# The mixer's output projection by seven products of eight, with its weight sums made ahead

## The chip, the core and the metric

The kernel runs on one core of one Trainium2 chip. The time is device microseconds of one execution. Five engines work beside each other, each through its own instructions in a fixed order: PE multiplies matrices, DVE and ACT do elementwise work, POOL does a little elementwise work and issues transfers that add into their target, SP issues the other loads. They meet through semaphores: an instruction that waits holds up everything behind it on its engine.

## The reference

One layer of a decoder trunk over 512 tokens of width 2048, each sub-layer with a norm ahead of it and a residual add behind:

```python
x = x + concat(dilated_attention, forgetting_attention, gated_linear_attention) @ w_out
x = x + cross_attention(rms_norm(x), rms_norm(mem)) # 256 memory tokens, 4 heads of 128
x = x + gated_mlp(rms_norm(x))                      # with a causal convolution of width 3
y = rms_norm(x)
```

All of it is float32. The change is in the product with `w_out` (2048 x 2048), in the sum of squares that the next norm needs, and in the preparation of the memory tokens for the cross-attention.

## The kernel before

Tokens lie along the free dimension, 512 of them, and features along 128 partitions: the stream is 16 tiles of 128x512 float32. To keep float32's accuracy each operand is split into a rounded high part and the rest (`whi` and `wlo` for weights: ACT makes the first, DVE the second), and one product is three matmuls: high by high, low by high and high by low (`mm3`, lines 375 to 377). Weights come as 512 KB loads on SP's queue into a ring of five (`wraw`); each load is split in two halves into rings of five `whi` and five `wlo`.

The output projection computes 16 output tiles, each from 16 blocks of the mixer's output: 16 x 3 matmuls of 512 columns a tile. The first four tiles take the first half of their blocks among the last steps of the attention; after it they take the second half, and tiles 4 to 15 follow whole (`out_units`, with `weights` at lines 361 and 362). A finished tile is added to the stream on DVE (`resid`, line 1073), squared on ACT (line 1094) and its square added to one of two sums `sq`, by POOL for even tiles and DVE for odd ones (line 1096; the first two squares by POOL at line 1090). From tile 8 on, each half tile is followed by a step of `memory`: it loads four blocks of memory tokens, splits them with their gain (lines 328 and 329), and adds up their squares in `msq`; its last two steps work out the norm (`stats`) and spread it over the partitions. Then `cross` multiplies the memory tokens by the key weights (PE on `mhi` and `mlo`) and the value weights.

The gated MLP's up projection works with seven products of eight already; sums of its weights that are used late are made ahead, in DRAM, by POOL's transfers: `up_sums(f)` issues eight of 512 KB, most of them adding and waiting for an earlier one. Sets 2 and 3 run in the attention (line 1316), set 1 behind `first_sums` (lines 1362 and 1366) in the cross-attention.

The order in which each engine runs its instructions comes from a scheduler over the program as it is written: it moves an instruction past others of its engine where it expects the engine free, so rows can stand far from where the code has them. On chip every engine then keeps that order.

Of the kernel before, what the change touches and what calls it, by code (L numbers as in the profile page):

```python
# [19 lines left out]
P = 128  # L20
# [33 lines left out]
EARLY = 4  # L54
BELOW = 3 * PHASE
# [28 lines left out]
H0 = 4  # L84
H1 = 6
ST = 4
# [89 lines left out]
def _pack(inp):  # L176
# [26 lines left out]
    a["w_o"] = _units_out(w_out, r(D))  # L203
# [30 lines left out]
class _Trunk:  # L234
# [200 lines left out]
    def stats(self, parts, n, name, pool=None):  # L435
# [8 lines left out]
        rs = self.con.tile([P, tl], F32, name="rs" + name)  # L444
        nc.vector.tensor_scalar(rs, ss[:, :tl], 1.0 / D, EPS, op0=ALU.mult, op1=ALU.add)
        nc.gpsimd.tensor_tensor(rs, rs, self.mhalf[:, :tl], op=ALU.pow)

        def spread():
            bc = self.pst("T")
            for t in range(tl):  # L450
                dg = (pool or self.pre).tile([P, P], F32, name="diag", tag="diag", bufs=tl)
                nc.vector.tensor_scalar(dg, self.ident, rs[:, t:t + 1], None, op0=ALU.mult)
                nc.tensor.matmul(bc[:, t * P:(t + 1) * P], self.ones, dg, start=True, stop=True)
            big = (pool or self.con).tile([P, n], F32, name="R", tag="R", bufs=1)
# [63 lines left out]
    def attend(self, qf, kf, e, vv, bias_of, head, mix):  # L518
# [17 lines left out]
        bias = bias_of(head)  # L536
# [344 lines left out]
    def mixer(self):  # L881
# [95 lines left out]
        for kl, o in zip(self.kl, (slice(DH, P), slice(0, DH))):  # L977
            nc.vector.memset(kl[o].bitcast(F32), 0.0)
        self.up_pre = {}
        for f in range(2, EARLY):  # L980
# [18 lines left out]

        def evac_o(dt):  # L1000
            def f(ps):
                self.resid(dt, ps, None, sqs, lambda n: self.mp.tile([P, n], F32, name="sqt", tag="sqt", bufs=2))
# [10 lines left out]
        units = [self.out_units(d["w_o"], n, xo, evac_o(n), box=box) for n in range(KT)]  # L1013
        self.rate = W_O / 2
        for n in range(0, 4, 2):
# [15 lines left out]
        self.flush()  # L1031
        es_ab.close()
# [4 lines left out]
        for n in range(4):  # L1037
            units[n][1]()
        mem = self.memory()
        for n in range(4, KT):  # L1040
            for u in units[n]:
                u()
                if n >= M0:
                    next(mem, None)
        for _ in mem:
            pass

    def memory(self):

        nc, mp = self.nc, self.mp  # L1050
        parts = [mp.tile([P, MEM], F32, name="msq%d" % i) for i in range(2)]
        self.mem = []
        for k in range(KT):
            if k % 4 == 0:
                four = mp.tile([P, 4, MEM], F32, name="mraw", tag="mraw", bufs=1)
                nc.sync.dma_start(out=four, in_=self.d["memT"][k // 4])
            raw = four[:, k % 4, :]
# [807 lines left out]
```

## Time and profile before

| | us |
|---|---|
| median of three runs | 2252.43 (2251.92 to 2252.64) |
| profiled execution | 2251.13 |
| its span | 2249.3 |
| PE busy | 2232.6 (99%) |
| DVE, ACT, POOL busy | 1819.5, 1231.7, 221.3 |
| window of tiles 4 to 15 | 707 to 837 |
| key units begin | 836.67 |

PE's busy time is nearly the span, so a window's length is what its matmuls take. A matmul's row shows a duration longer than the distance to the next, since matmuls overlap; the distance between starts is what counts. In the rows of DVE the same holds to a small part. Where the profile names the releaser of a wait, it is the one that came last.

### The profile page before, as it was taken

How to read it: one execution, taken by the hardware profiler on the slowest of the kernel's cores; microseconds unless marked ns; L12 is line 12 of the kernel's file. 1: busy time of each engine (PE TensorE's matmuls, PEld its weight loads, DVE VectorE, ACT ScalarE, POOL GpSimd, SP SyncE). 2: the span in 40 equal slices, each digit the busy share in tenths (PEclk: the TensorE clock that was granted, in tenths of full speed). 3: DMA queues.
4: the chain of work that ended last, by engine and by line, in shares of the span. 5: the costliest groups of instructions: out<-in, count | busy, mean ns of one | idle time of the engine just before them, and what ended most of it. 6: DMA issues, size and time to landing. Idle time of an engine off the chain costs nothing.

```text
span 2249.3 us, 42619 instructions
## 1 busy us (share of the span) xinstructions
PE 2232.6 (99%) x15898; PEld 2089.9 (93%) x15898; DVE 1819.5 (81%) x3587; ACT 1231.7 (55%) x2532; POOL 221.3 (10%) x308
## 2 busy tenths in 40 slices
PE   9999999999999999999999999999999999999997
PEld 8898898888888888889999999999999999999997
DVE  7826756666787356699999999999999999989887
ACT  7324445555575245585555555555555575747563
POOL 2000101000002011121111111111000020101003
PEclk9999999999999999999999999999999999999999
DMA  6422157222224359589777777877534493837542
GB/s 223 162 96 82 49 150 193 97 89 99 78 92 140 122 161 241 134 206 282 198 212 201 221 208 213 215 219 224 173 132 144 145 344 104 305 124 233 186 129 82
DMA packets 141842, 377.09 MB, mean 168 GB/s; under 512 B 14484, under 2 KB 53732, under 8 KB 140932
## 3 DMA queue, kind: packets, MB, share of 16 engines
q1 hardware_dynamic: 90144, 274.18, 35.1%
q0 software_dynamic: 45728, 89.86, 18.2%
q10 hardware_dynamic: 5764, 10.35, 1.3%
q8 instruction: 124, 2.03, 0.4%
q14 instruction: 82, 0.67, 0.1%
HBM read 347.28 MB, written 91.80 MB: 195 GB/s over the span
## 4 chain that ended last, share of the span: by engine, by line
PE 96%; DVE 2%; ACT 1%; DMA 0%; issue 0%; POOL 0%; SPq 0%; DVEq 0%; ACTq 0%
PE acc L375 19%; PE acc L377 19%; PE acc L376 19%; PE psC L375 5%; PE psC L376 5%; PE psC L377 5%; PE acc L416 3%; PE acc L418 3%; PE acc L417 3%; PE psD L377 3%; PE psD L376 3%; PE psD L375 3%; PE psT L556 1%; PE psQ L377 1%; PE psQ L375 1%; PE psQ L376 1%
## 5 line engine op out<-in xcount | busy, mean ns | idle before, releaser
L336 ACT ACTIVATE whi<-wraw 128x512 fp32r<-128x512 f32 (+1 forms) x822 | 471.1, 603 | 407.3 <-PE acc L376 145.0
L337 DVE TENSOR_TENSOR wlo<-wraw,whi 128x512 fp32r<-128x512 f32 (+1 forms) x822 | 522.3, 656 | 65.9 <-ACT whi L336 61.2
L375 PE MATMUL acc<-sum,whi 128*128 128x256 f32 x1956 | 541.8, 277 | 0.4 <-ACT s L1465 0.3
L377 PE MATMUL acc<-sum,wlo 128*128 128x256 f32 x1956 | 541.5, 277 | 0.0
L376 PE MATMUL acc<-sum,whi 128*128 128x256 f32 x1956 | 541.4, 277 | 0.0
L362 DVE TENSOR_TENSOR wlo<-wraw,whi 128x512 fp32r<-128x512 f32 (+2 forms) x328 | 216.1, 665 | 191.2 <-ACT whi L361 188.8
L375 PEld LDWEIGHTS acc<-sum,whi 128*128 128x128 f32 x1956 | 367.2, 188 | 1.0 <-ACT s L1465 0.8
L377 PEld LDWEIGHTS acc<-sum,wlo 128*128 128x128 f32 x1956 | 367.3, 188 | 0.4 <-DVE wlo L337 0.2
L376 PEld LDWEIGHTS acc<-sum,whi 128*128 128x128 f32 x1956 | 367.3, 188 | 0.1
L361 ACT ACTIVATE whi<-wraw 128x512 fp32r<-128x512 f32 (+2 forms) x328 | 198.5, 610 | 284.3 <-PE acc L376 186.5
L375 PE MATMUL acc<-xhi,whi 128*128 128x512 f32 (+1 forms) x848 | 335.1, 395 | 0.5 <-ACT fg L926 0.5
L377 PE MATMUL acc<-xhi,wlo 128*128 128x512 f32 (+1 forms) x848 | 328.4, 387 | 0.0
L376 PE MATMUL acc<-xlo,whi 128*128 128x512 f32 (+1 forms) x848 | 327.9, 387 | 0.0
L375 PE MATMUL psC<-sum,whi 128*128 128x256 f32 x928 | 256.9, 277 | 0.0
L376 PE MATMUL psC<-sum,whi 128*128 128x256 f32 x928 | 256.8, 277 | 0.0
L377 PE MATMUL psC<-sum,wlo 128*128 128x256 f32 x928 | 256.5, 276 | 0.0
L377 PEld LDWEIGHTS acc<-xhi,wlo 128*128 128x128 f32 x848 | 159.3, 188 | 32.5
L375 PEld LDWEIGHTS acc<-xhi,whi 128*128 128x128 f32 x848 | 159.4, 188 | 29.9 <-ACT fg L926 0.9
L376 PEld LDWEIGHTS acc<-xlo,whi 128*128 128x128 f32 x848 | 159.7, 188 | 29.0 <-DVE xlo L324 0.2
L377 PEld LDWEIGHTS psC<-sum,wlo 128*128 128x128 f32 x928 | 174.3, 188 | 0.0
L375 PEld LDWEIGHTS psC<-sum,whi 128*128 128x128 f32 x928 | 174.3, 188 | 0.0
L376 PEld LDWEIGHTS psC<-sum,whi 128*128 128x128 f32 x928 | 174.2, 188 | 0.0
(401 smaller groups left out, 4319.0 us busy)
## 6 DMA issues: line engine op xcount, KB each, us to landing
wraw<-in_w_up SPq DMA_DIRECT2D x125, 512.0 KB, 6.3
b<-in_w_up SPq DMA_DIRECT2D x42, 512.0 KB, 4.5
wraw<-in_w_o SPq DMA_DIRECT2D x32, 512.0 KB, 3.5
wraw<-in_w_d SPq DMA_DIRECT2D x32, 448.0 KB, 4.3
wraw<-in_w_d SPq DMA_DIRECT2D x36, 384.0 KB, 5.0
wraw<-in_w_qka SPq DMA_DIRECT2D x24, 512.0 KB, 3.5
up<-in_w_up POOLq DMA_DIRECT2D x24, 512.0 KB, 7.0
one<-in_w_d POOLq DMA_DIRECT2D x24, 448.0 KB, 6.7
```

What stands on the lines that cost most here:

```text
L336: nc.scalar.activation(hi, r, AF.Copy)
L337: nc.vector.tensor_tensor(lo, r, hi.bitcast(F32), op=ALU.subtract)
L361: nc.scalar.activation(hi, r, AF.Copy)
L362: nc.vector.tensor_tensor(lo, r, hi.bitcast(F32), op=ALU.subtract)
L375: nc.tensor.matmul(out, lh, rh, start=start, stop=False, skip_group_check=more)
L376: nc.tensor.matmul(out, lh, rl, start=False, stop=False, skip_group_check=more)
L377: last = nc.tensor.matmul(out, ll, rh, start=False, stop=stop, skip_group_check=more)
L416: self.nc.tensor.matmul(o, xh[:, tt], wh, start=(k == 0), stop=False)
L417: self.nc.tensor.matmul(o, xh[:, tt], wl, start=False, stop=False)
L418: self.last = self.nc.tensor.matmul(o, xl[:, tt], wh, start=False, stop=(k == KT - 1))
L556: nc.tensor.transpose(tp[:, b * P:(b + 1) * P], pt[:, b * P:(b + 1) * P], self.ident)
```

## The change

Four tiles stay as they were. The other twelve are three `quad`s of four tiles. A quad is two pairs of output tiles; a pair is computed from 2 x 2 blocks (two output tiles, halves of the 512 tokens, pairs of input blocks) by seven products instead of eight. Each product is 8 x 3 matmuls of 256 columns. It needs sums of weight blocks and sums of token blocks:

- `out_sums` makes the weight sums in DRAM ahead of time: 32 transfers of POOL, 384x512 (786 KB) each, in the attention, in front of `up_sums` 2, 3 and now also 1.
- `token_turns` makes the token sums: subtractions and splits on DVE and ACT, in steps between the products of the first two quads.
- `quad` multiplies, and puts the products together with adds on DVE and ACT; a tile is ready only after several products, and its residual add goes into a list (`todo`) that is worked off among the next products.
- The squares of these tiles are added to `sq` by an adding transfer of POOL (line 1188) instead of POOL's or DVE's adds.
- `memory` runs among the products of the last quad. It loads two blocks at a time, and the squares from the third on are added into two tiles `low` by adding transfers of POOL (line 1273). `stats` for it is called after the second of the key units, and its last step after the fourth; the keys' evacuations wait in a list until then.
- `attend` issues a head's bias load two heads ahead.

On DVE, at the end of the last quad and the start of the key units (`wlo` of line 344 are weight halves of the quad, of line 369 the key units'; `tok` the split memory tokens; `vg` partial tiles; `low<-low` the add of `stats` over the memory's squares):

```order
1241 L344 TENSOR_TENSOR wlo<-wraw,whi 128x512 [waits DVE_49,DMAHW3_49,PE_49,Activation_49]
1242 L344 TENSOR_TENSOR wlo<-wraw,whi 128x512 [waits PE_49,Activation_49]
1243 L448 TENSOR_TENSOR low<-low 128x256 [waits DMASW4_49,DMASW3_49]
1244 L344 TENSOR_TENSOR wlo<-wraw,whi 128x512 [waits DMAHW7_49,PE_49,Activation_49]
1245 L1168 TENSOR_TENSOR vg<-vg,s_6888 128x256 [waits Activation_49]
1246 L1168 TENSOR_TENSOR vg<-s_6888,acc 128x256 [waits DMASW7_49]
1247 L336 SCALAR_TENSOR_TENSOR xlo<-str,gains,xhi 128x512 [waits Activation_49]
1248 L1168 TENSOR_TENSOR vg<-vg,s_6889 128x256 [waits DVE_49]
1249 L344 TENSOR_TENSOR wlo<-wraw,whi 128x512 [waits PE_49,Activation_49]
1250 L1168 TENSOR_TENSOR str<-xraw,vg 128x512 [waits DMAHW1_49,DVE_49]
```

The add of `stats`, which the code calls in the key units, stands ahead of the quad's last six weight halves, and waits for two transfers of POOL. Before, the same add on DVE:

```order
1108 L329 SCALAR_TENSOR_TENSOR mlo_7586<-mraw,gains,mhi_7585 128x256
1109 L329 SCALAR_TENSOR_TENSOR mlo_7593<-mraw,gains,mhi_7592 128x256 [waits Activation_49]
1110 L1096 TENSOR_TENSOR msq_7367<-msq_7367,msqt 128x256 [waits DVE_49,Activation_49]
1111 L441 TENSOR_TENSOR msq_7366<-msq_7366,msq_7367 128x256 [waits DVE_49,Pool_49]
1112 L362 TENSOR_TENSOR wlo<-wraw,whi 128x512 [waits PE_49,Activation_49]
```

It stood right behind the last square's add of its own engine. On POOL the memory's squares are now these transfers (`low<-spare`), with the stream's (`sq<-vg`) between and behind them:

```order
112 L1273 DMA low<-spare 128x256 [waits DMASW6_49]
113 L1188 DMA sq_6461<-vg 128x512 [waits DMASW7_49,Activation_49]
114 L1273 DMA low<-spare 128x256 [waits DMASW0_49,Activation_49]
115 L1273 DMA low<-spare 128x256 [waits DMASW4_49,DMASW1_49,Activation_49]
116 L1273 DMA low<-spare 128x256 [waits DMASW3_49,Activation_49]
117 L1273 DMA low<-spare 128x256 [waits DMASW4_49,Activation_49]
118 L1273 DMA low<-spare 128x256 [waits DMASW5_49,Activation_49]
119 L1273 DMA low<-spare 128x256 [waits DMASW6_49,Activation_49]
```

Each of them waits for the landing (a semaphore DMASW) of the one two places before it in its kind, as both add into the same tile; before, each place was an add on POOL or DVE that waited for ACT's square.

The diff, with the parts that the prediction speaks of; the token sums' arithmetic is cut:

```diff
+PLAIN = 4
+QUADS = (KT - PLAIN) // 4
+LAST_ORDER = (5, 6, 3, 7, 1, 2, 4)
+OUT_ORDER = (1, 2, 4, 5, 6, 3, 7)
...
     def attend(...):
+            if f is turn and t == 1:
+                n = self.heads.index(me) + 2
+                if n < len(self.heads):
+                    name, h = self.heads[n]
+                    self.biases[name, h] = getattr(self, name)(h)
...
-        for f in range(2, EARLY):
+        self.out_sums()
+        for f in (2, 3, 1):
             self.up_sums(f)
...
-        mem = self.memory()
-        for n in range(4, KT):
-            for u in units[n]:
-                u()
-                if n >= M0:
-                    next(mem, None)
-        for _ in mem:
-            pass
+        mem = self.mem_steps = self.memory()
...
+        for c in range(QUADS):
+            last = c == QUADS - 1
+            if last:
+                next(mem)
+            self.quad(PLAIN + 4 * c, LAST_ORDER if last else OUT_ORDER, mem if last else turns,
+                      c == QUADS - 2)
+        while self.todo:
+            self.todo.popleft()()
+        self.mem_rest = mem
...
+    def quad(self, d0, order, steps, swap):
...
+        def out(o, i):
...
+            tt(x1, raw, t, ALU.subtract if i else ALU.add)
+            nc.scalar.activation(t, x1, AF.Square)
+            nc.gpsimd.dma_start(out=self.sqs[i], in_=t, accum_op=ALU.add)
...
+        for n, j in enumerate(order):
+            for o in pairs:
+                s1, s5 = o["s1"], o["s5"]
+                parts = self.halves(self.up_raw(o["src"][j]))
...
+                ps = bank(o, where[j])
+                for i in range(NP):
+                    th, tl = parts[i // 4]
+                    c = slice(i % 4 * P, (i % 4 + 1) * P)
+                    self.mm3(ps, th[:, c], tl[:, c], *self.operand(j, i), i == 0 and j not in (2, 3, 7),
+                             i == NP - 1, more=True)
...
     def memory(self):
...
+        parts = [self.low(MEM, F32) for _ in range(2)]
         for k in range(KT):
...
+            if k < 2:
+                nc.scalar.activation(parts[k], raw, AF.Square)
+            else:
+                sq = self.spare([P, MEM])
+                nc.scalar.activation(sq, raw, AF.Square)
+                nc.gpsimd.dma_start(out=parts[k % 2], in_=sq, accum_op=ALU.add)
...
     def cross(self):
...
         for i, u in enumerate(first):
             more((i >= H0) + (i >= H1))
+            if i in (2, 4):
+                next(self.mem_rest)
+            if i == 4:
+                ready.append(True)
+                for f, ps in keys:
+                    f(ps)
             u()
...
+    def out_sums(self):
+        w, n = self.d["w_p"], (KT - PLAIN) // 4
+        self.out_src = []
+        for g in range(2):
+            t = [self.dr.tile([n * P, 1024], F32, name="wo%d%d" % (g, i)) for i in range(4)]
+            b11, _, b22, b21 = b = [w[i, g * n:(g + 1) * n].rearrange("k p c -> (k p) c") for i in range(4)]
+            cuts = [slice(512 * h, 512 * (h + 1)) for h in range(2)]
+            self.added(*[[[x[:, c] for c in cuts] for x in y] for y in (t, b)])
```

`added` is the chain that `up_sums` used already: a first copy, then adds into it, each issued behind the one before on POOL's queue; it now takes lists of pieces.

More of the change, by code (lines that the diff above doesn't have):

```diff
@@ L978, in mixer @@
             nc.vector.memset(kl[o].bitcast(F32), 0.0)
+        self.biases = {}
+        self.heads = [("bias_a", h) for h in range(A_HEADS)] + [("bias_b", h) for h in range(B_HEADS)]
         self.up_pre = {}
-        for f in range(2, EARLY):
+        self.out_sums()
+        for f in (2, 3, 1):
             self.up_sums(f)
@@ new lines, in mixer @@
+        self.mem_left = KT // 2
+        for n in range(PLAIN):
+            w = self.weights(d["w_o"][2 * n + 1])
+            for kk in range(8):
+                wh, wl = w(kk * P, P)
+                self.mm3(box[n], wh, wl, *xo[8 + kk], False, kk == 7)
+            if n == PLAIN - 2:
+                turns = self.token_turns([self.mix[m] for m in order], xo)
+                for _ in range(4):
+                    next(turns)
+        for n in range(PLAIN):
+            evac_o(n)(box[n])
+        for c in range(QUADS):
[4 more added lines that the diff above has]
+                      c == QUADS - 2)
@@ L1052, in memory, with load @@
+    def memory(self):
+        nc = self.nc
+        def load(k):
+            two = self.spare([P, 2, MEM])
+            nc.sync.dma_start(out=two, in_=self.d["memT"][k // 4, :, k % 4:k % 4 + 2, :])
+            return two
+        loads = [load(0), load(2)]
         self.mem = []
+        yield
+        parts = [self.low(MEM, F32) for _ in range(2)]
         for k in range(KT):
-            if k % 4 == 0:
-                four = mp.tile([P, 4, MEM], F32, name="mraw", tag="mraw", bufs=1)
-                nc.sync.dma_start(out=four, in_=self.d["memT"][k // 4])
@@ L1057, in memory @@
-            raw = four[:, k % 4, :]
-            hi = mp.tile([P, MEM], F32R, name="mhi%d" % k)
-            lo = mp.tile([P, MEM], F32R, name="mlo%d" % k)
-            self.mem.append(self.split_to(hi, lo, raw, self.gain(4, k)))
-            self.square(k, raw, parts, lambda n: mp.tile([P, n], F32, name="msqt", tag="msqt", bufs=2))
-            if k % 4 == 3:
+            if k % 2 == 0:
+                two = loads.pop(0)
+            raw = two[:, k % 2, :]
+            both = self.ring()
+            self.mem.append(self.split_to(both[:, :MEM], both[:, MEM:], raw, self.gain(4, k)))
@@ L1116, in evac_k @@
             return f
[L1118 to L1119 removed]
+        ck = [self.spare([P, S], F32R) for _ in range(X_HEADS)]
+        vh = [self.spare([P, S], F32R) for _ in range(MT)]
+        vl = [self.spare([P, S], F32R) for _ in range(MT)]
         def evac_v(t, ps):
```

221 lines of the change are left out of this document (179 added, 42 removed).

## The prediction

> **What bounds the kernel now.** I read the page's busy time and chain first, then a table of stages, then the groups, the timeline and the queues of the stages that the change touches.
>
> ```profile
> span 2249.3 us, 42619 instructions
> PE 2232.6 (99%) x15898; PEld 2089.9 (93%) x15898; DVE 1819.5 (81%) x3587; ACT 1231.7 (55%) x2532; POOL 221.3 (10%) x308
> PE 96%; DVE 2%; ACT 1%; DMA 0%; issue 0%; POOL 0%; SPq 0%; DVEq 0%; ACTq 0%
> ```
>
> PE is idle for 16.7 us of 2249.3 (2249.3 - 2232.6), and the chain that ended last is 96% PE. So only two things move the end: PE work taken out or put in, and any new time in which PE waits. The stages (window, its length, then busy time of PE, PEld, DVE, ACT, POOL, the granted clock, the DMA engines' share, GB/s):
>
> ```profile
> 307.00:395.00 88.00, 87.78 (x443) 75.17 (x441) 56.20 (x139) 48.68 (x108) 13.26 (x17) 1.00 0.73 192
> 604.00:690.00 86.00, 85.69 (x429) 69.98 (x427) 70.58 (x203) 56.11 (x137) 0.00 (x0) 1.00 0.26 90
> 707.00:837.00 130.00, 130.00 (x580) 107.84 (x579) 58.48 (x93) 50.42 (x90) 15.63 (x16) 1.00 0.42 143
> 837.00:854.00 17.00, 17.00 (x143) 16.81 (x142) 14.88 (x26) 13.11 (x23) 1.04 (x1) 1.00 1.02 270
> 1010.00:1800.00 790.00, 789.60 (x6935) 789.21 (x6934) 754.90 (x1225) 439.95 (x789) 80.66 (x105) 1.00 0.69 199
> ```
>
> The twelve tiles of the change are 707 to 837: PE is full there and DVE idle for more than half of it, the shape in which fewer products should pay. The memory's key units follow (837 to 854), PE full again, so a delay made before them isn't made up behind.
>
> **The change part by part.**
>
> *Fewer products.* The spacing of matmuls, from PE's timeline where the last tile of 512 columns ends and the key units of 256 begin (start, duration):
>
> ```profile
> 834.63 0.39 PE L375 MATMUL acc<-xhi,whi 128*128 128x512 f32 x1
> ...
> 836.67 0.28 PE L375 MATMUL acc<-mhi,whi 128*128 128x256 f32 x1
> ...
> 841.15 0.28 PE L377 MATMUL acc<-mhi,wlo 128*128 128x256 f32 x1
> ```
>
> Nine of 512 columns lie between the first two rows: 2.04/9 = 226.7 ns. Before, 12 tiles x 16 x 3 = 576 of them: 130.6 us. Now 3 quads x 14 products x 8 x 3 = 1008 of 256 columns. For their spacing there are two rows: the long up stage of 256-column products, 789.60/6935 = 113.9 ns, and the key units, 38 from 836.67 to 841.15, 117.9 ns. I take 113.9, since token sums against split weights are what the up stage multiplies too: 114.8 us. **Gain 15.8 us**; by the key units' spacing it would be 11.8.
>
> *What the products need on DVE and ACT.* A weight half costs PE 12 x 113.9 ns = 1.37 us now. DVE writes per half one `wlo`, and beside it the token sums' subtractions and splits in the first quad. Durations and spacing:
>
> ```profile
> L362 DVE TENSOR_TENSOR wlo<-wraw,whi 128x512 fp32r<-128x512 f32 x48 | 32.7, 687 | 47.2 <-ACT whi L361 47.2
> L361 ACT ACTIVATE whi<-wraw 128x512 fp32r<-128x512 f32 x48 | 30.0, 629 | 69.6 <-PE acc L376 69.5
> L1096 DVE TENSOR_TENSOR msq<-msq,msqt 128x256 f32<-128x256 f32 x4 | 1.6, 412 | 0.0
> L1094 ACT ACTIVATE msqt<-mraw 128x256 f32<-128x256 f32 x8 | 3.2, 402 | 0.0
> 838.18 0.68 DVE L362 TENSOR_TENSOR wlo<-wraw,whi 128x512 fp32r<-128x512 f32 x1
> 838.78 0.74 DVE L329 SCALAR_TENSOR_TENSOR xlo<-str,gains,xhi 128x512 fp32r<-128x512 f32 x1
> 839.44 0.68 DVE L1096 TENSOR_TENSOR sq<-sq,sqt 128x512 f32<-128x512 f32 x1
> 840.05 0.68 DVE L362 TENSOR_TENSOR wlo<-wraw,whi 128x512 fp32r<-128x512 f32 x1
> ```
>
> Operations queued back to back start 0.60 us apart for `wlo`, 0.66 for `xlo`, 0.61 for an add: 0.08 less than their durations, so a 128x256 one goes at about 0.33. In the first quad DVE's order has per half one `wlo` and mostly a 128x256 and a 128x512 of the tokens: 0.60 + 0.33 + 0.60 = 1.53 against 1.37, for some ten halves. The ring of five split halves lends up to 5 x 1.37 = 6.8 us, so between 0 and 3 us show. I take **1 us lost**. ACT's half costs 0.63 and has room.
>
> *Weight sums ahead.*
>
> ```profile
> L1316 POOL DMA_DIRECT2D up<-in_w_up x24: 611/1015/1112, 307.7 to 1590.6; - x24
> 691.67 1.42 POOL L1090 TENSOR_TENSOR sq<-str 128x512 f32<-128x512 f32 x1 [302.42 <-DVE str L1073]
> ```
>
> Before, 16 POOL transfers of 512 KB (8.4 MB, two sets of sums) fill 307.7 to 395; the engines' share rises there from 0.26 (row of 604) to 0.73: 0.47 x 88 = 41 us of all sixteen, 4.9 us per MB. The new 32 transfers move 25.2 MB, 124 us of all sixteen; in the 0.74 that is free, 167 us. Three sets of the up sums follow at 44 us each. End: 307 + 167 + 132 = 606 us. POOL's next work, behind all of these in its queue, is the first square, before at 691.67 after 302.42 us without work. If each 786 KB transfer ran alone at 1.5 x 5.5 us (88/16, scaled by size), it would be 307 + 264 + 132 = 703. DVE needs the squares in its first quad at about 709 (two POOL operations of 1.4 us and an add before that), so even this doesn't show. Slower loads do not either: at 837 to 854 the share was 1.02 and PE was busy for all 17.00 us. Cost 0; its cover is the 85 us between 606 and 691. The biases two heads ahead: PE was idle 0.31 us in 604 to 690, so they are worth nothing.
>
> *Squares by DMA.* The adds of the stream's squares leave POOL and DVE; neither was on the path there (15.63 and 58.48 us of 130), so they are worth nothing by themselves. The memory's fourteen adds become two chains of seven POOL transfers (128x256, 128 KB), each waiting for the one two before it, since they add into the same two tiles. Their sum is read by one DVE add, the first step of `stats`. In DVE's order that add stands behind 22 of the last quad's 28 weight halves: six more `wlo`, the evacuations and the key units' first half are queued behind it. The nearest rows are the stream's accumulating transfers of 128x512 (256 KB) in the cross-attention's output:
>
> ```profile
> L1254 POOL DMA_DIRECT2D sq<-xsqt x14: 862/872/907, 956.0 to 996.6; - x14
> DMA to landing us min/median/max: 3.3/4.7/7.2
> 977.03 0.86 POOL L1254 DMA_DIRECT2D sq<-xsqt  x1 [1.47 <-ACT xsqt L1253]
> 978.58 0.86 POOL L1254 DMA_DIRECT2D sq<-xsqt  x1 [0.68 <-ACT whi L336]
> 983.68 0.87 POOL L1254 DMA_DIRECT2D sq<-xsqt  x1 [4.24 <-DMA sq<-xsqt]
> 986.18 0.87 POOL L1254 DMA_DIRECT2D sq<-xsqt  x1 [1.62 <-DMA sq<-xsqt]
> ```
>
> Where a link waited for its own chain, the period was 983.68 - 977.03 = 6.65 and 986.18 - 978.58 = 7.60 us. Issuing is 0.87 of it and doesn't shrink; half of the rest for half of the bytes gives 3.76 and 4.24. I take **c = 4.0 us** a link, since these two rows are the only ones of two chains that run against each other. Low end: the least landing, 3.3, halved, with the issue: 2.5. High end: the median landing, 4.7, not shrunk, with the issue: 5.6.
>
> The stall, from t0, PE's start of the last quad (14 products of 2.73 us, so its end is t0 + 38.3). The two tiles of partial sums lie where the quad's first two products read a token sum: free at t0 + 5.5, then an evacuation and two squares on ACT, 0.4 each: first transfer at t0 + 6.7, the second chain 0.9 behind it, the last landing at t0 + 7.6 + 7c. After it DVE has to run, in its order, 7 `wlo` (0.60), 7 operations of 128x256 (0.33), 2 residual adds (0.60) and 6 `xlo` (0.66) before the key units' first half is there: 4.2 + 2.3 + 1.2 + 4.0 = 11.7 us. PE starts the key units at t0 + 19.3 + 7c in place of t0 + 38.3: lost 7c - 19.0, **9.0 us at c = 4.0**, nothing below c = 2.7, 20.2 at c = 5.6. SP is held too: its loads of the later memory blocks wait for links of the chain, and the last three weight loads of the quad stand behind the load that waits for the third link:
>
> ```profile
> wraw<-in_w_o SPq DMA_DIRECT2D x32, 512.0 KB, 3.5
> ```
>
> Freed at t0 + 7.6 + 3c = t0 + 19.6 and landed 3.5 later, they are there well before PE's twelfth product at t0 + 30, so this hides behind the products. DVE has 14.88 of 17 us to do in the key units, so it keeps up there but wins nothing back.
>
> The Trainium skill, "DMA: Bandwidth & Descriptors", section "Anatomy of one DMA — SWDGE (gpsimd) path", fits a transfer as about 2.0 us plus bytes at 436 GB/s. By that, an estimate, a link of 128 KB takes 2.3 us and this sum would hold no stall. For 256 KB it gives 2.6, and the fourteen here landed in 3.3 to 7.2, so this trace does not bear it out.
>
> *Sum.* -15.8 + 1 + 9 = -5.8 us. The profiled execution took 2251.13 (span 2249.3 and 1.8 around it), so 2245.3; the median of the runs, 2252.43, is 1.3 above it: **2246.6 us**.
>
> **The rivals.**
>
> *The chain is short.* If landings are like the quiet ones, c = 2.5, DVE finds the sums there and only the first quad costs: 2252.4 - 15.8 + 0 to 1 = 2237. For it: the share in 707 to 837 is 0.42, and the accumulates were measured in a busier stretch. Against it: this quad loads 512 KB every 2.73 us, 192 GB/s, more than the 143 there, and the two chains contend with each other.
>
> *The chain eats the gain.* Same place: if a link costs what a 256 KB one does (c = 5.6) the loss is 20.2 and the kernel comes out at 2252.4 - 15.8 + 1 + 20.2 = 2257.8, slower. It decides from 7c - 19 = 14.8, c = 4.8: above that the chain takes all that the products gave. For it: medians near 4.7 at twice the size suggest that much of a landing doesn't depend on bytes. Against: the two chain-bound rows scaled as above.
>
> *Half-width products aren't half as long.* At the key units' 117.9 ns the gain is 11.8, the last quad is 39.6 us long and the stall 7.7: 2252.4 - 11.8 + 1 + 7.7 = 2249.3, no change that can be told. For it: those units also have 256 columns against split weights. Against: 6935 records at 113.9.
>
> *The sums arrive late.* From an end of about 706 on, every microsecond holds POOL's squares, then DVE and PE. 32 transfers at 10 us each would end at 307 + 320 + 132 = 759, some 50 us lost: 2290. Nothing in the rows asks for it unless transfers in pairs hinder each other.
>
> **How the numbers follow.** About 0.2%, 4.5 us, is what a measurement here can tell from no change. Forecast (c from 3.4 to 4.6, 2242 to 2251): 0.50. Short chain: 0.22. Long chain: 0.16. Wide spacing: 0.07. Late sums: 0.05. Faster by over 4.5 us, below 2247.9: the short chain and some two thirds of the forecast, 0.56. Within: the other third, the wide spacing and a part of the long chain, 0.27. Slower: the rest of the long chain and late sums, 0.17. The range runs from no stall to c = 5.5: 2237 to 2257; the forecast's own is 2242 to 2251.
>
> **What would show it.** In the trace of the changed kernel: matmuls of the quads 113 to 114 ns apart, and the out projection's PE time near 115 us. One wait on DVE at the memory's sum (`low<-low`), released by a DMA, of some 10 us, and PE idle right behind it, before the key units: about 9 us. The starts of `low<-spare` on POOL two apart by c: 4.0. The weight sums ended near 606 and POOL's first square not later than before. It would be wrong if DVE reaches that add when the chain has landed (c under 2.7), if PE idles in the first quad by more than 3 us, or if the idle time sits in the attention.

## The result and the profile after

The changed kernel takes 2269.55 us (median of six runs, 2264.13 to 2270.98); the kernel before, beside it, 2251.78 us (2251.25 to 2252.64). The ratio is 1.0075, with an interval of 1.0064 to 1.0086: 17.8 us slower. The prediction was 2246.6 us, with a range of 2237 to 2257. The profiled execution of the change is the fastest of its six, 2264.13 us with a span of 2262.3, so its trace holds 13.0 us of the 17.8 (2262.3 - 2249.3).

The page of the changed kernel, its span, busy times and the engines of the chain that ended last:

```profile
span 2262.3 us, 43896 instructions
PE 2228.4 (99%) x16330; PEld 2105.9 (93%) x16330; DVE 1861.5 (82%) x3692; ACT 1266.7 (56%) x2610; POOL 272.0 (12%) x351
PE 61%; DMA 2%; DVE 1%; ACT 1%; issue 0%; POOL 0%; DVEq 0%; ACTq 0%; POOLq 0%
```

PE's busy time fell by only 4.2 us, and its idle time rose from 16.7 to 33.9 us (2262.3 - 2228.4). The chain has 2% of DMA now: work released by a transfer, where before 96% was PE. (Its shares add up to 65% because the profile follows it back from the end to 789.61 us only, into the last quad.)

The points at which PE reaches the same place of the program show where the time went. In the changed kernel PE starts the first quad, the last quad, the memory's key units and the first 512-column product behind the value units at:

```profile
708.81 0.28 PE L382 MATMUL acc<-xhi,whi 128*128 128x256 f32 x1
...
788.78 0.29 PE L382 MATMUL psC<-tok,whi 128*128 128x256 f32 x1
...
848.24 0.29 PE L382 MATMUL acc<-tok,whi 128*128 128x256 f32 x1
...
897.98 0.39 PE L382 MATMUL acc<-xhi,whi 128*128 128x512 f32 x1
```

Before, the twelve tiles and the first 512-column product behind the value units began at

```profile
705.20 0.39 PE L375 MATMUL acc<-xhi,whi 128*128 128x512 f32 x1
...
882.63 0.39 PE L375 MATMUL acc<-xhi,whi 128*128 128x512 f32 x1
```

and the key units at 836.67. Between the first of these rows and the key units lie 576 matmuls of 512 columns, and eight small ones of the memory's norm (four at 775.92, four at 781.81) that take 0.9 us of the first eight tiles. In the changed kernel these eight stand in the key units.

| stretch | before | after | difference |
|---|---|---|---|
| up to the twelve tiles (attention and four plain tiles) | 705.2 | 708.8 | +3.6 |
| first eight tiles / two quads | 88.0 | 80.0 | -8.0 |
| last four tiles / last quad | 43.5 | 59.5 | +15.9 |
| key and value units | 46.0 | 49.7 | +3.8 |
| the rest | 1366.7 | 1364.3 | -2.4 |
| span | 2249.3 | 2262.3 | +13.0 |

Two quads win; the third takes back twice as much. The stages of the last quad in the changed kernel (window, its length, busy time of PE, PEld, DVE, ACT, POOL, granted clock, DMA share, GB/s):

```profile
788.80:805.00 16.20, 16.20 (x144) 16.20 (x143) 11.77 (x23) 12.71 (x30) 5.02 (x6) 1.00 0.95 255
805.00:815.00 10.00, 6.74 (x42) 6.02 (x41) 4.83 (x10) 4.18 (x10) 3.68 (x5) 0.85 1.04 290
815.00:825.00 10.00, 7.00 (x51) 6.21 (x50) 4.11 (x8) 5.80 (x14) 3.70 (x5) 0.98 0.67 150
825.00:835.00 10.00, 6.11 (x36) 5.76 (x36) 1.56 (x3) 5.46 (x11) 3.26 (x4) 0.83 0.71 159
835.00:845.00 10.00, 7.53 (x44) 7.53 (x44) 8.61 (x18) 4.68 (x9) 0.88 (x1) 0.66 0.47 112
845.00:848.20 3.20, 3.20 (x29) 3.20 (x28) 3.20 (x7) 2.47 (x6) 0.87 (x1) 1.00 1.03 352
```

From 805 to 845 PE works 27.4 of 40 us and all other engines have room as well. PE's busy time over the stage is 16.2 + 27.4 + 3.2 = 46.8 us, and the quad needs 39.4 undisturbed (worked out further down). So of the 20.1 us lost there, 12.6 are idle time and 7.4 are matmuls that ran slower. The granted clock fell where they did; by these rows it makes up some 4.8 of the 7.4 (6.74 x 0.15 + 7.00 x 0.02 + 6.11 x 0.17 + 7.53 x 0.34, an estimate), and what the rest is stays open.

Who stopped whom. PE's three long waits in the quad:

```profile
811.71 0.39 PE L382 MATMUL acc<-xhi,whi 128*128 128x256 f32 x1 [3.04 <-ACT whi L343]
824.20 0.39 PE L382 MATMUL acc<-xhi,whi 128*128 128x256 f32 x1 [2.61 <-ACT whi L343]
837.48 0.58 PE L384 MATMUL acc<-xhi,wlo 128*128 128x256 f32 x1 [6.36 <-DVE wlo L344]
```

The first two wait for ACT's upper weight halves (`whi`), the third for DVE's lower ones (`wlo`). On ACT, just ahead of those halves:

```profile
810.72 0.42 ACT L1272 ACTIVATE spare<-spare 128x256 f32<-128x256 f32 x1 [4.10 <-DMA low<-spare]
...
823.21 0.42 ACT L1272 ACTIVATE spare<-spare 128x256 f32<-128x256 f32 x1 [2.97 <-DMA low<-spare]
```

A square (line 1272) waits until the transfer of an earlier square has landed, because its result goes into one of the eight `spare` tiles (the loads of the memory's tokens use the same ring) and a transfer holds its tile until then. And on DVE the add of `stats`:

```profile
836.39 0.42 DVE L448 TENSOR_TENSOR low<-low 128x256 f32<-128x256 f32 x1 [9.70 <-DMA low<-spare]
```

So the same chain stops PE in two ways: first through ACT, from 808.7 on, then through DVE, which waits from 826.7 to 836.4.

### The profile page after: what moved, and what is told of

Read it like the earlier page. It is cut to its first block, busy times and chain, and to the rows that moved or that the text cites. A ratio compares the mean times of both kernels' runs of the same rounds, so it can differ in the third digit from the quotient of the medians.

```text
span 2262.3 us, 43896 instructions
## 1 busy us (share of the span) xinstructions
PE 2228.4 (99%) x16330; PEld 2105.9 (93%) x16330; DVE 1861.5 (82%) x3692; ACT 1266.7 (56%) x2610; POOL 272.0 (12%) x351
## 4 chain that ended last, share of the span: by engine, by line
PE 61%; DMA 2%; DVE 1%; ACT 1%; issue 0%; POOL 0%; DVEq 0%; ACTq 0%; POOLq 0%
PE acc L384 11%; PE acc L382 11%; PE acc L383 11%; PE psC L382 5%; PE psC L383 5%; PE psC L384 5%; PE psD L382 3%; PE psD L384 3%; PE psD L383 3%; DMA low<-spare 1%; PE psQ L382 1%; PE psQ L383 1%; PE psQ L384 1%; DMA sq<-vg 0%; PE acc L424 0%
## 5 line engine op out<-in xcount | busy, mean ns | idle before, releaser
L343 ACT ACTIVATE whi<-wraw 128x512 fp32r<-128x512 f32 (+2 forms) x906 | 522.9, 605 | 435.9 <-PE acc L383 159.3
L344 DVE TENSOR_TENSOR wlo<-wraw,whi 128x512 fp32r<-128x512 f32 (+2 forms) x906 | 578.6, 658 | 95.0 <-ACT whi L343 86.7
L382 PE MATMUL acc<-xhi,whi 128*128 128x512 f32 (+1 forms) x800 | 303.8, 380 | 6.4 <-ACT whi L343 5.6
L384 PE MATMUL acc<-xhi,wlo 128*128 128x512 f32 (+1 forms) x800 | 297.6, 372 | 7.0 <-DVE wlo L344 6.8
L383 PE MATMUL acc<-xlo,whi 128*128 128x512 f32 (+1 forms) x800 | 296.4, 371 | 0.0
L369 DVE TENSOR_TENSOR wlo<-wraw,whi 128x512 fp32r<-128x512 f32 (+2 forms) x280 | 182.2, 658 | 135.3 <-ACT whi L368 133.1
L368 ACT ACTIVATE whi<-wraw 128x512 fp32r<-128x512 f32 (+2 forms) x280 | 167.7, 606 | 204.1 <-PE acc L383 107.0
L384 PEld LDWEIGHTS acc<-xhi,wlo 128*128 128x128 f32 x800 | 153.0, 191 | 33.4 <-DVE wlo L344 8.3
L382 PEld LDWEIGHTS acc<-xhi,whi 128*128 128x128 f32 x800 | 153.0, 191 | 29.6 <-ACT whi L343 6.1
L383 PEld LDWEIGHTS acc<-xlo,whi 128*128 128x128 f32 x800 | 153.2, 191 | 21.5 <-DVE xlo L331 0.3
```

What stands on the lines that cost most here:

```text
L343: nc.scalar.activation(hi, r, AF.Copy)
L344: nc.vector.tensor_tensor(lo, r, hi.bitcast(F32), op=ALU.subtract)
L368: nc.scalar.activation(hi, r, AF.Copy)
L369: nc.vector.tensor_tensor(lo, r, hi.bitcast(F32), op=ALU.subtract)
L382: nc.tensor.matmul(out, lh, rh, start=start, stop=False, skip_group_check=more)
L383: nc.tensor.matmul(out, lh, rl, start=False, stop=False, skip_group_check=more)
```

## Experiments

Times are medians; the kernel before, measured beside each, took 2252.1 to 2252.2 us. "Last quad" and the like are the stretches of the table above in the experiment's profiled execution.

### The memory's squares added by POOL

```diff
             sq = self.spare([P, MEM])
             nc.scalar.activation(sq, raw, AF.Square)
-            nc.gpsimd.dma_start(out=parts[k % 2], in_=sq, accum_op=ALU.add)
+            nc.gpsimd.tensor_tensor(parts[k % 2], parts[k % 2], sq, op=ALU.add)
```

> The changed kernel with the memory's fourteen squares added by POOL's elementwise adds (some 0.75 us each) instead of adding transfers; all else kept. Theory (the chain of transfers holds DVE, ACT and SP): the last quad takes 40 to 44 us from its first matmul to the key units' first instead of 59.5, the kernel 2249 to 2256 us instead of 2269.5. Rival (the quads are slow by themselves, by the matmuls' spacing or the clock): the last quad stays above 55 us and the kernel above 2264.

Measured: 2253.94 us, ratio 1.0009 (0.9997 to 1.0022), and the last quad 43.8 us in place of 59.5. Of the 17.8 us, 15.6 went with these fourteen transfers (2269.55 - 2253.94): they are the main cause. What is left is no gain, so something else eats the products' share too.

### The add of `stats` put later, the chain kept

```diff
-        nc.vector.tensor_tensor(a, a, b, op=ALU.add)
+        if new:
+            with self.tc.issue_after(self.cut.ins):
+                nc.vector.tensor_tensor(a, a, b, op=ALU.add)
+        else:
+            nc.vector.tensor_tensor(a, a, b, op=ALU.add)
```

`cut` is the last weight half split so far; the add now stands on DVE where the code calls it, in the key units.

> The chain of transfers kept, but DVE's add of the two sums pinned behind the weight splits of the second key unit, where the code has it. Theory A (what counts is that the add stands ahead of six weight halves): no PE idle time between product twelve and the key units, the kernel 15 to 20 us below the changed one, 2250 to 2255. Rival B (ACT's squares and SP's loads wait for the chain through the ring of eight spare tiles, whatever DVE does): PE still idle for 8 to 14 us in the last quad, the kernel only 3 to 8 us lower, 2262 to 2267.

Measured: 2264.88 us, 1.0053 (1.0036 to 1.007). The last quad took 51.7 us, the key and value units 54.9. PE's waits in the stretches 800 to 860 and 845 to 905 of this kernel (what waited for what: total, times, longest):

```profile
PE acc L382 <- ACT whi L343: 5.8, 4, 2.8
...
PE psT L464 <- DVE low L463: 6.2, 1, 6.2
```

With DVE's wait out of the quad, 12.3 us are still lost there (51.7 - 39.4), and PE's waits in it are mostly for ACT. The wait for the sum came back in the key units, as 6.2 us for the norm. So the place of DVE's add, on which the prediction had hung the whole loss, is worth 4.7 us by the medians (2269.55 - 2264.88). Against the first experiment, which has no such chain, 7.9 us are lost in the quad through ACT and slower matmuls (51.7 against 43.8) and 4.4 in the key and value units, where the sum is still late (54.9 against 50.5). No run gave the ring of `spare` tiles more room by itself.

### The weight sums left out

```diff
-            t = [self.dr.tile([n * P, 1024], F32, name="wo%d%d" % (g, i)) for i in range(4)]
...
-            self.added(*[[[x[:, c] for c in cuts] for x in y] for y in (t, b)])
...
-                                     5: t[0][rows], 6: t[1][rows], 4: t[2][rows], 7: t[3][rows]})
+                                     5: b[1][rows], 6: b11[rows], 4: b22[rows], 7: b21[rows]})
```

> The changed kernel without the 32 transfers that make the weight sums: the quads load single blocks of the weights in place of the sums, so the product is another one; the up sums start where those were. Theory (the attention lost 2.7 us to slower bias loads beside them): the quads start near 706.6 as before the change instead of 709.3, DVE waits under 5 us for biases instead of 13, the kernel 2 to 4 us lower, 2265.5 to 2267.5. Rival (the delay is from the order of the biases two heads ahead): DVE's wait stays near 13 us and the time within 1 us.

Measured: 2262.49 us, 1.0045 (1.003 to 1.006), 7.1 us less than the change, more than the 2 to 4 expected. (The two profiled executions differ by 2.2 us only; that of the change was its fastest.) The twelve tiles start at 705.2, as before the change. The stage 307 to 604 (columns as in the table of stages), in the kernel before:

```profile
307.00:604.00 297.00, 296.41 (x1459) 248.59 (x1458) 195.67 (x517) 165.88 (x387) 13.26 (x17) 1.00 0.40 121
```

in the changed kernel:

```profile
307.00:604.00 297.00, 294.29 (x1449) 246.78 (x1448) 193.80 (x511) 164.44 (x383) 56.76 (x51) 1.00 0.86 209
```

and without the sums:

```profile
307.00:604.00 297.00, 296.49 (x1461) 248.86 (x1460) 195.67 (x518) 166.00 (x387) 19.53 (x25) 1.00 0.48 135
```

The DMA share is 0.86 with the sums, and PE works 2.1 us less there than before; without them it works as long as before. That the sums cost time in the attention is shown. One way in which they do is DVE's add to a head's bias, waiting for the bias's load. These waits took 3.8 us in the kernel before. DVE's waits in 500 to 690 in the changed kernel (total, times, longest):

```profile
DVE ba L609 <- DMA ba<-cdr: 13.0, 6, 3.5
```

and without the sums:

```profile
DVE ba L609 <- DMA ba<-cdr: 3.2, 5, 1.3
```

### The operands of the products moved by 64 bytes

The spacing of the quads' matmuls was not the forecast's one number: products on `xhi`/`xlo` run at 120.0 ns, those on token sums at 113.8. This run moved tiles by pads (`PHASE` is 16 columns of 4 bytes, 64 bytes a pad), meant to move `xhi` and `xlo` alone, and changed nothing else:

```diff
+                if k == 0:
+                    self.xp.tile([P, PHASE], F32, name="shelf")
...
+                if not hasattr(self, "shift"):
+                    self.shift = self.vvp.tile([P, PHASE], F32, name="shift")
...
+        if not hasattr(self, "rest"):
+            self.rest = self.kv.tile([P, PHASE], F32, name="rest")
```

> The changed kernel with the split token blocks xhi and xlo moved by 64 bytes in SBUF, so that they no longer start at the same offset from a multiple of 128 bytes as the weights' halves; every other tile keeps its offset. Theory (a 256-column matmul whose moving and stationary operand have the same offset goes at 119.8 ns instead of 113.9): the quads' products on x go at 114, 576 x 5.9 ns = 3.4 us less in the quads, of which some disappears in the last quad's stall; the first two quads 2.2 us shorter. Rival (the spacing hangs on something else): it stays at 119.8. The products of 512 columns may get slower; if they do it shows outside the quads.

Measured: 2275.14 us, 1.0095 (1.0078 to 1.0113). In the changed kernel, a product on x, one on sums, and the start of the next (48 matmuls from the first row to the second, 48 from the third to the fourth):

```profile
720.83 0.28 PE L382 MATMUL psC<-xhi,whi 128*128 128x256 f32 x1
...
726.59 0.29 PE L382 MATMUL psC<-tok,whi 128*128 128x256 f32 x1
...
732.11 0.28 PE L382 MATMUL acc<-tok,whi 128*128 128x256 f32 x1
...
737.57 0.28 PE L382 MATMUL psC<-tok,whi 128*128 128x256 f32 x1
```

5.76/48 = 120.0 ns on x, 5.46/48 = 113.8 on sums. With the tiles moved, the same four rows, and then 55 products of 512 columns on x behind the value units, from the fifth row to the last:

```profile
727.70 0.28 PE L382 MATMUL psC<-xhi,whi 128*128 128x256 f32 x1
...
733.13 0.28 PE L382 MATMUL psC<-tok,whi 128*128 128x256 f32 x1
...
738.71 0.28 PE L382 MATMUL acc<-tok,whi 128*128 128x256 f32 x1
...
744.36 0.28 PE L382 MATMUL psC<-tok,whi 128*128 128x256 f32 x1
...
907.31 0.39 PE L382 MATMUL acc<-xhi,whi 128*128 128x512 f32 x1
...
920.13 0.36 PE L382 MATMUL psS<-spare,cqh 128*128 128x256 f32 x1
```

113.1 ns on x, as the theory asked, but 116.3 and 117.7 on sums (48 matmuls each), and 12.82/55 = 233.1 ns at 512 columns. In the changed kernel those 55 run from 897.98 to

```profile
910.47 0.38 PE L382 MATMUL psS<-spare,cqh 128*128 128x256 f32 x1
```

at 12.49/55 = 227.1. So the spacing changed with the pads alone: what helps the products of 256 columns on x hurts those of 512 columns on the same tiles, and those on sums. The pads were to leave the sums' tiles in place against a multiple of 128 bytes, and no record shows where each tile lies, so the theory of equal offsets is not shown. As a remedy the move is worse than nothing.

### All squares of these tiles added by POOL

To the first experiment's edit, the stream's squares (line 1188):

```diff
             nc.scalar.activation(t, x1, AF.Square)
-            nc.gpsimd.dma_start(out=self.sqs[i], in_=t, accum_op=ALU.add)
+            self.pooled = nc.gpsimd.tensor_tensor(self.sqs[i], self.sqs[i], t, op=ALU.add)
```

> As e1_pool_adds (the memory's squares added by POOL), and the stream's squares of the twelve tiles too: no adding transfer is left in the quads. Theory (in e1 POOL still waits for the stream's chain, first ahead of the memory's adds, then ahead of the norm's power that the keys need): the last quad goes from 43.8 to about 40 us, PE's wait for the norm in the key units (2.8 us in e1) goes, the kernel 3 to 7 us below e1's 2253.9, at 2247 to 2251. Rival (those chains are hidden): within 1.5 us of e1.

Measured: 2251.83 us, 1.0000 (0.9991 to 1.0009); the last quad 44.7 us, where about 40 was expected, the key and value units 48.0 us in place of 50.5 in the first experiment. In the changed kernel POOL's last transfer of the stream's chain, behind which the power of the memory's norm is queued, was

```profile
859.89 0.86 POOL L1188 DMA_DIRECT2D sq<-vg  x1 [7.72 <-DMA sq<-vg]
```

and PE stood 2.1 us for the norm (2.5 in the first experiment). With POOL's adds that wait is 0.7, and against the change 1.7 of the 3.8 us that the key and value units had lost come back (49.7 to 48.0). It is the norm's place behind the stream's chain on POOL, not work of DVE.

### Biases loaded further ahead, and not ahead at all

Two runs on the biases. One, with the first experiment's edit, issues the second group's biases four heads ahead, two of them into tiles that are free there; the other is the change without its own bias loads ahead.

```diff
-                n = self.heads.index(me) + 2
-                if n < len(self.heads):
+                m = self.heads.index(me)
+                for n in [m + 2] * (m + 2 < A_HEADS + 2) + [m + 4] * (A_HEADS + 2 <= m + 4 < len(self.heads)):
...
-        cb = self.ab.tile([P, S], F32, name="ba", tag="ba", bufs=2)
+        if h % 4 < 2:
+            cb = self.ab.tile([P, S], F32, name="ba", tag="ba", bufs=2)
+        else:
+            cb = self.con.tile([P, S], F32, name="bq%d" % (h % 2), tag="sq%d" % (h % 2))
```

> As e1_pool_adds, with the forgetting heads' biases loaded four heads ahead into four buffers (two of them the still unused sums of squares), not two heads ahead into two. Theory (beside the weight sums a bias takes up to 10 us to land, DVE waits for it, PE runs dry and its clock drops): DVE's wait for biases falls from 13 to 17 us to under 6, the quads start at 706 to 709 in every run, the kernel 4 to 7 us below e1, at 2247 to 2250, with less spread. Rival (the attention is slowed by something else under the transfers, such as weight loads): quads still start after 711.

```diff
-            if f is turn and t == 1:
-                n = self.heads.index(me) + 2
-                if n < len(self.heads):
-                    name, h = self.heads[n]
-                    self.biases[name, h] = getattr(self, name)(h)
```

> The changed kernel without the bias loads two heads ahead: each head loads its own, as before the change. Theory (the loads ahead take a part of the landing off, but little): DVE waits longer for biases, 20 us or more, and the kernel is 2 to 6 us above the changed one, 2271 to 2276. Rival (the loads ahead are worth nothing, as forecast): within 1.5 us of 2269.5.

Measured: 2255.85 us (1.0014, 1.0003 to 1.0026) and 2269.12 us (1.0075, 1.006 to 1.009). Without the loads ahead the kernel takes what the change takes: they are worth nothing. With biases four heads ahead DVE's waits for them fell from 17.4 us in the first experiment's trace to 10.8 (7.9 for the old tiles, 2.9 for the new ones), not under 6 as expected, and the median did not fall with them (2255.85 against 2253.94). So the waits for biases exist, and one of them stopped PE for 3.26 us in the first experiment's trace, but that they carry all of the attention's loss is not shown.

### All repairs together

POOL's adds for both kinds of squares, the later add of `stats`, and the biases four heads ahead (edits as shown):

> Everything that helped together: all squares by POOL's adds, DVE's add of the memory's sums behind the second key unit, biases four heads ahead. If the three losses (chain 16 to 20, norm's wait 2 to 3, attention 3 to 10) are the whole difference, the kernel shows what the products give less the spacing of the products on x: 2252 - 12 = 2240, with 2237 to 2244 as the range. If something else in the quads costs, it stays above 2246.

Measured: 2251.43 us (2245.98 to 2258.43), 1.0002 (0.9992 to 1.0013); the expectation was missed. The last quad took 44.5 us, still 5.1 more than its own 39.4, and in the profiled execution (2256.91 us) the twelve tiles started at 717.1, the latest start of any profiled run. Three runs took this apart.

First, the sums' transfers one at a time, and one set of the up sums back to its old place:

```diff
-        for f in (2, 3, 1):
+        for f in (2, 3):
...
-            self.added(*[[[x[:, c] for c in cuts] for x in y] for y in (t, b)])
+            for c in cuts:
+                self.added(*[[[x[:, c]] for x in y] for y in (t, b)])
...
+        self.up_sums(1)
         return src
```

> As e8_best, with the weight sums' transfers one behind the other instead of two in flight, and the first set of up sums back in the cross-attention, so that the sums still end before POOL's squares. Theory (it is the full DMA engines, 0.85 to 0.9 busy from 307 to 604, that make the biases late): the share falls to about 0.7, the quads start at 706 to 709 in place of 717.6, the kernel 3 to 8 us below e8's 2251.4, at 2243 to 2248. Rival (any such transfer beside the attention costs the same, whatever the number in flight): the quads start after 711, the kernel within 2 us of e8.

Second, no weight sums at all (the edit of the third experiment):

> As e8_best without the weight sums' transfers (the quads load single blocks, so the product is another one). It shows what is left when the attention pays nothing: quads start at 705 to 707, last quad 44 to 45 us, the kernel at 2241 to 2246. If the attention's loss is not from these transfers, it stays at 2249 or above.

Third, without the memory's squares and their adds from the third block on:

```diff
-            else:
-                sq = self.spare([P, MEM])
-                nc.scalar.activation(sq, raw, AF.Square)
-                nc.gpsimd.tensor_tensor(parts[k % 2], parts[k % 2], sq, op=ALU.add)
```

> As e8_best without the memory's last fourteen squares and their adds (the memory's norm is left wrong). e8's last quad takes 44.5 us, 5 above its matmuls' own 39.4. Theory A (POOL's adds slow DVE's operations beside them, and DVE's order is full): the last quad falls to 40 to 41.5 us and the kernel by 3 to 5 us, to 2246.5 to 2248.5. Theory B (DVE's own work of the quad is too long for it): it stays above 43.

Measured: one at a time 2250.88 us (0.9998, 0.9988 to 1.0008); no sums 2246.19 us (2245.54 to 2248.42; 0.9974, 0.9964 to 0.9985); no squares of the memory 2243.24 us (0.9967, 0.9954 to 0.998). With one transfer at a time the DMA share of 307 to 604 fell only from 0.85 to 0.79, and the median moved by some 0.5 us, as the rival said, though the quads started at 707.9 in the profiled execution. Taking the sums away moves it by 5.2 (2251.43 - 2246.19), and the runs then lie within 3 us of each other in place of 12. So the sums cost 5 to 7 us in both ways of queueing them that were tried: 7.1 in the third experiment, 5.2 here.

Without the memory's squares and adds the last quad takes 39.6 us, its own PE time, 4.8 less; the median fell by 8.2, and the difference was not followed up. What held the quad is seen in DVE's groups of the stretch 788 to 834, the splits of the memory's tokens (16 operations; busy time, mean ns, and idle time ahead of them). In the changed kernel:

```profile
L336 DVE SCALAR_TENSOR_TENSOR tok<-spare,gains,tok 128x256 fp32r<-128x256 f32 x16 | 7.3, 479 | 1.1 <-ACT tok L335 1.1
```

with POOL's adds for the memory alone (the first experiment):

```profile
L336 DVE SCALAR_TENSOR_TENSOR tok<-spare,gains,tok 128x256 fp32r<-128x256 f32 x16 | 11.3, 733 | 0.9 <-ACT tok L335 0.9
```

with all repairs, and below it an evacuation:

```profile
L336 DVE SCALAR_TENSOR_TENSOR tok<-spare,gains,tok 128x256 fp32r<-128x256 f32 x16 | 13.9, 895 | 0.0
...
L1175 DVE TENSOR_TENSOR vg<-psC,vg 128x256 f32<-128x256 f32 x6 | 2.5, 418 | 0.4
```

and with all repairs, but no adds of the memory:

```profile
L336 DVE SCALAR_TENSOR_TENSOR tok<-spare,gains,tok 128x256 fp32r<-128x256 f32 x16 | 9.2, 602 | 0.0
```

POOL's adds stretch DVE's splits from 479 to 895 ns. In the timeline with all repairs the 13 splits that run beside an add of POOL take 0.96 us on average, the other three 0.44. So DVE becomes the bound of the quad: with all repairs it is busy for 44.42 of the last quad's 44.45 us and PE waits for its `wlo`, and without the memory's adds it is busy for 38.16 of 39.61. The evacuation, which reads one of its operands from PSUM, takes 418 ns there and 420 in the change. The Trainium skill ("SBUF — State Buffer", section "Who interferes with whom") says that a VectorE instruction with two SBUF inputs contends with a GpSimd instruction that reads SBUF, and that one with at most one SBUF input, outside the two-port modes, does not; the two rows of that trace agree.

### The memory's squares added by DVE

So the adds were given to the engine that would be stretched by POOL: DVE adds the memory's squares and those of the last quad's own tiles, the first two quads keep the transfers, the sums go one at a time, and the later add and the biases stay (the edit is against the run with the transfers one at a time):

```diff
-            self.pooled = nc.gpsimd.tensor_tensor(self.sqs[i], self.sqs[i], t, op=ALU.add)
+            if steps is self.mem_steps:
+                nc.vector.tensor_tensor(self.sqs[i], self.sqs[i], t, op=ALU.add)
+            else:
+                nc.gpsimd.dma_start(out=self.sqs[i], in_=t, accum_op=ALU.add)
...
-                nc.gpsimd.tensor_tensor(parts[k % 2], parts[k % 2], sq, op=ALU.add)
+                nc.vector.tensor_tensor(parts[k % 2], parts[k % 2], sq, op=ALU.add)
```

> As e9_serial, with the memory's squares and those of the last quad's tiles added by DVE, and those of the first two quads by transfers as in the change: no elementwise add of POOL beside the last quad, no chain that the last quad waits for. Theory (in e8 and e9 POOL's adds stretch DVE's operations, 895 ns for a 128x256 split against 602 with the memory's adds left out; fourteen adds on DVE itself cost 14 x 0.33 = 4.6 us): the last quad falls from 44.5 to 39.5 to 41.5 us, the kernel 3 to 6 us below e9's 2250.9, at 2245 to 2248, and below the kernel before. Rival (DVE is then full by itself): the last quad stays above 43.5 us and the kernel above 2249.5.

Measured: 2248.51 us (2244.41 to 2255.37), ratio 0.9986 (0.9977 to 0.9996): the only kernel of the study that computes everything and whose interval lies below 1, by 3.6 us, less than the 0.2% that the prediction counts as a difference. It falls just short of what was expected (2245 to 2248, and a last quad of 39.5 to 41.5). The last quad takes 42.2 us, the key and value units 47.3, and the splits are back at

```profile
L336 DVE SCALAR_TENSOR_TENSOR tok<-spare,gains,tok 128x256 fp32r<-128x256 f32 x16 | 7.5, 482 | 1.7 <-ACT tok L335 1.7
```

## Why the prediction was wrong, step by step

The terms of its sum beside what the profiled execution shows:

| step | predicted | measured |
|---|---|---|
| Fewer products | -15.8 | -12.3 |
| What the products need on DVE and ACT | +1 | +1.1 |
| Squares by DMA, the last quad | +9.0 | +20.1 |
| Squares by DMA, key and value units | 0 | +3.8 |
| Weight sums ahead, with the biases | 0 | +3.6 here, 5 to 7 by medians |
| the norm's small matmuls, gone from the tiles | 0 | -0.9 |
| the rest, not explained | 0 | -2.4 |
| sum | -5.8 | +13.0 |

**Fewer products: right in kind, mis-sized.** The 1008 matmuls are 576 on x and 432 on token sums (of the seven products, four read x and three read sums). At the rows above they take 576 x 120.0 + 432 x 113.8 = 118.3 us: 12.3 us less than the 130.6 before, and 39.4 a quad. The prediction took one spacing, that of the up stage, for both. Its rival of half-width products had the size nearly right (11.8) for a reason that fits half of it: the products on x are the ones spaced wider.

**First quad: right in size, in part by luck.** Two quads need 78.9 us and took 80.0. But only some 0.5 of it lies in the first quad (96 matmuls on x in 708.81 to 720.83, 12.02 us for 11.52), and as much in the second (144 in 743.07 to 760.79, 17.72 us for 17.28), where the one wait that the profile names, of 0.2 us, is for ACT and not for DVE.

**Squares by DMA: right place, wrong size, and one mechanism left out.** This is the step that failed most. The stall sat where the prediction put it, and its formula held: the last landing was forecast at t0 + 7.6 + 7c, and the add ran at 836.39 = t0 + 47.6, so c = 40.0/7 = 5.7 us a link. By 7c - 19.0 that is 21 us, and 20.1 were lost. The size c = 4.0 came from halving the bytes' part of the 256 KB rows. The fourteen transfers of 128 KB landed in

```profile
DMA to landing us min/median/max: 2.6/5.1/9.4
```

against 3.3/4.7/7.2 for twice the bytes: halving the bytes did not make them shorter. In the last quad itself both sizes stand side by side (size, median us from issue to landing):

```profile
low<-spare POOLq DMA_DIRECT2D x14, 128.0 KB, 5.1
sq<-vg POOLq DMA_DIRECT2D x6, 256.0 KB, 5.5
```

The rival in which the chain eats the gain had put its high end at 5.6, the unhalved row, and named the point from which it decides, c = 4.8; it is the one that came true in this step, though its total, 2257.8, is 11.7 us below the median for the other steps. The 5.7 is an average and not the price of a bare link: five of the fourteen issues waited last for a landing, six for ACT, and the first two links took 8.6 us (795.79 to 804.38) and some 9.2 (about 797.0 to 806.20).

By the fit of the Trainium skill ("DMA: Bandwidth & Descriptors", section "Anatomy of one DMA — SWDGE (gpsimd) path") a link would have taken 2.3 us, an estimate; the row does not agree for this stage, whose DMA share was 0.47 to 1.04.

What the step left out is ACT. It named DVE and SP as waiting for the chain; but each square of ACT also needs a `spare` tile that a landing sets free, and the weight halves stand behind it in ACT's order. PE was stopped through ACT from 808.7 and from 821.6, before DVE had even reached its add (826.7), and with that add moved away 12.3 us of the loss stayed. That the formula gives the sum nearly right, with c read off a chain that ACT's waits had stretched and with only half of the mechanism in it, is in part luck.

**The clock was not priced.** In five-microsecond stretches of the last quad's end the changed kernel shows (columns as above, the granted clock third from the end):

```profile
810.00:815.00 5.00, 3.17 (x14) 2.86 (x15) 2.42 (x5) 2.56 (x6) 1.72 (x2) 0.70 1.00 239
825.00:830.00 5.00, 5.00 (x29) 4.86 (x30) 1.56 (x3) 5.00 (x11) 1.53 (x2) 0.66 0.96 227
835.00:840.00 5.00, 2.52 (x12) 2.53 (x13) 3.60 (x8) 0.00 (x0) 0.00 (x0) 0.59 0.18 26
```

After a wait of 2.6 to 6.4 us PE comes back at 0.6 to 0.7 of its clock for some microseconds: by the estimate above some 4.8 of the 7.4 us of slower matmuls. The Trainium skill ("TensorE: Matmul & The Clock Gate", section "HAM oscillation — how this bites in real kernels") has the rule that PE must not idle for more than about 3.4 us or its clock is halved. The trace agrees roughly; the first two of these falls stand behind waits of 3.04 and 2.61 us, somewhat under that figure.

**Key and value units: "wins nothing back", but loses more.** The step looked at DVE there. What came late was the power of the memory's norm on POOL, queued behind the stream's chain that the same edit had made: 2.1 of the 3.8 us are PE's wait for it, 0.8 are the norm's own small matmuls, which stand here now, and the rest goes with a clock of 0.97 over the stretch. With POOL's adds the stretch fell to 48.0 us.

**Weight sums ahead: "cost 0" was wrong.** The sums were not late for POOL: the first square started at 698.11 (691.67 before) and waited for DVE, not for them. The last transfer of the up sums was issued at 637.19; the forecast had them ended at 606. The failed sentence is "slower loads do not either", which rested on a stage with share 1.02 and a full PE. In 307 to 604 PE worked 2.1 us less at a share of 0.86. One loss seen in the attention is DVE's wait for bias loads, 13.0 us in place of 3.8; that it carries all of it is not shown. That stage's own order, with biases loaded shortly before DVE needs them, would have had to be looked at, not another stage with the same share.

**Biases: right.** Without their loads ahead nothing changes (2269.12).

## What to carry to other kernels

An accumulate by transfer that adds into the same tile is a chain of landings, and every engine that lends it a buffer joins that chain: list who waits for each tile that a transfer holds, the producers for its ring as well as the reader of its sum, before calling it hidden. Price a link by measured landings and the issue, unscaled (4.7 + 0.87 was 5.6 here; 5.7 came on average, with ACT's waits in it), and add to PE's waits the slower matmuls behind them, here 7.4 us for 12.6 of waiting. An algorithm with fewer products gives only what its own operands' spacing allows, and its extra sums and adds have to be paid on engines that the same stage loads: of the 15.8 us on paper, 3.6 were left in the best version.

## What the runs showed of the hardware that was not expected

- The spacing of fp32 matmuls changes with the place of tiles: with pads of 64 bytes 256-column products on x went from 120.0 to 113.1 ns, those on token sums from 113.8 to 116.3 and 117.7, and 512-column products from 227.1 to 233.1. No run says why.
- Accumulating transfers of 128 KB landed hardly sooner (median 5.1 us) than ones of 256 KB beside them (5.5), and no sooner than such ones in another stage (4.7), so a chain of them pays by link.
- POOL's adds of two tiles slow DVE's two-operand work beside them: a 128x256 split from 479 to 895 ns on average.
- Transfers that fill 0.86 of the DMA engines cost a stage bound by PE 0.7% of its time (2.1 of 297 us) in one execution, and in the repaired kernel they spread the runs over 12 us; without them the runs lie within 3 us.
